# A two-block transformer layer in split fp32: VectorE makes the low weight parts that GpSimd made

## The chip, the cores and the metric

One core of one Trainium2 chip, one launch. The metric is the device time of one execution in microseconds (us); of several runs the median is given. In the profile PE is TensorE's matmul, PEld its weight load, DVE is VectorE, ACT is ScalarE, POOL is GpSimd, and SP is SyncE, which issues most of the DMAs. A small q (SPq, POOLq) marks the queue of an engine.

## The reference, cut to what matters

256 tokens of width 1024, all in fp32, pass through two blocks.

The first block: layer norm; one projection into queries, keys and values of two attentions and into two gates; an 8-head neighbourhood attention and an 8-head windowed attention with a sink; each through its branch matrix; the gated sum

```
mixed = sigmoid(ga) * y_na + sigmoid(gb) * y_swa
h = layer_norm(ALPHA * h + mixed @ w_out + b_out)
h = layer_norm(ALPHA * h + square(relu(h @ w_ff1 + b_ff1)) @ w_ff2 + b_ff2)
```

The second block has two layers. The first mixes by pooling (a trailing mean over 2, 4, 8 or 16 tokens minus the token, then a 256 x 256 matrix for each channel group), the second by a 16-head windowed attention with shared keys and values. After each mixer stands a feed-forward network: a matrix to 2 x 2816 channels, a causal convolution of width 3, gelu(gate) * value, and a matrix back. Norms are RMS norms.

## The kernel before, in words

**Products in three parts.** TensorE runs on a rounded type (fp32r). To keep fp32 accuracy, each weight chunk and each activation is split: the high part is the value rounded to fp32r, the low part is the value minus its high part. A product is the sum of three matmuls, high x high, high x low, low x high (mm3, L364 to L369; in Tm.run, L414 to L432, the order is high x high over all of the contraction, then low weights, then low activations).

**Weights.** The host lays all weights out as 268 chunks of 128 x 1024 in the order of their use. The class Weights (L76 to L175) is the pipeline: load (L91) issues a chunk's DMA on SyncE's queue into a raw buffer; high (L118) makes the high part on ScalarE (L131), and returns a function low, which makes the low part (L141) on the engine that it is given, VectorE by default, then counts the chunk as done and calls load for the next one. There are four raw buffers, and two lent ones at the beginning, so that a load waits for the low part that frees its buffer. For seven chunks a gain is folded in by L129 and L138 instead, always on ScalarE and VectorE. high and low parts live in slots: seven at first (NW), later nine and one extra. take hands the next split chunk to the matmuls, free gives the slot back, and pump(most, eng, keep) splits as many next chunks as there are free slots, most at most, with the low parts on engine eng. highs(n) makes only high parts and leaves the calls of the low parts to the caller.

**Order.** The schedule is written out by hand (manual_schedule): each engine runs its instructions in the order in which the program emits them. An engine that waits for a semaphore holds all its later instructions. So where a low part is called decides what stands behind it on its engine.

**Stages, in order of time.**
- Start: the layer norm ln0 (L495 to L501) of each 128-token half; between the statistics and the centring (L279) it calls mid, which makes the low part of chunk 0. to_fm (L357) transposes on TensorE (L348), copies the high part on ScalarE and subtracts on VectorE (both in split_out, L337 to L339). Tm.run makes the first projections.
- First attention: unit_a (L371 to L388) computes 256 output channels for all tokens; f_va (L569) the values. Scores, softmax and value products are interleaved with the other projections as fillers (step, L727), the branch projection f_bna (L627) among them.
- Branch mixing: the second branch matrix with swa_epi (L766 to L779): L770 reads a PSUM bank, L772 adds two SBUF tensors, ScalarE writes the high part (L775), L777 the low part. Here unit_a is called with ahead=1: high parts are made before the epilogue, low parts after it, for the second half (m = 1) on GpSimd.
- Output projection: Acc.both and Acc.tail (L466 to L489), in which post_ln and to_fm of the first half stand between matmuls; tail's fills names the engines of four low parts. The vector loads of GpSimd's queue (vec, L217) follow the second norm.
- Feed-forward of the first block: GpSimd computes rotary angles meanwhile (rope_angles, L817).
- Pool mixer (L984 to L1071): residual addition L331, scaling L322, transposes, with five low parts between them.
- conv_ffn (L1074 to L1122) for layer 0 and 1: the units 3 to 5 call unit_a with one low part after each half; epilogue L1085 (ScalarE), L1086, L1088, L1093 and the split (VectorE). Four banks rotate, so the matmuls of a unit wait until L1088 of the unit two before has read its bank.
- Second attention (L1204 to L1353): at its end wo is applied to the second half of the tokens, with pump after each chunk (L1351).

The 36 low parts on GpSimd are: chunks 0, 2 and 4 at the start; 10; 13, 15, 17 and 18 in f_va; 31 to 34 in f_bna; 44, 46, 47 and 48 in the branch mixing; 53 in the output projection; 116, 117, 119, 121 and 122 in the pool mixer; 129 to 134 and 214 to 219 in the two conv_ffn; 204 and 206 at the end of the second attention.

Of the kernel before, what the change touches and what calls it, by code (L numbers as in the profile page):

```python
# [177 lines left out]
def model(tc, x_in, wts, bvec, cols_in, const_in, nab_in, pos_in, out):  # L178
    nc = tc.nc
    from contextlib import ExitStack  # L180
    with ExitStack() as top:
# [189 lines left out]
        def unit_a(kx, epi, nk=8, pump=(2, None), ahead=0):  # L371

            cs = [W.take(4, 256) for _ in range(nk // 4)]
            for m in range(2):
                o = bank()
                for k in range(nk):
                    c = cs[k // 4]
                    mm3(o[:, :T], [c[i][:, k % 4, m * P:(m + 1) * P] for i in range(2)], kx(k),
                        k == 0, k == nk - 1, True)
                    if m == 1 and k % 4 == 3:  # L380
                        W.free(cs[k // 4])
                lows = W.highs(ahead)
                later = epi(m, o) or ()
                for low in lows:
                    low((nc.vector,nc.gpsimd)[m])
                W.pump(0 if ahead else pump[0], pump[1], keep=KEEP)
                for f in later:
                    f()  # L388
# [113 lines left out]

        ln0(0, lambda: lows.pop(0)(nc.gpsimd))
        to_fm(x_t[0], xT, 0)
        lows.pop(0)()
        W.pump(1, nc.gpsimd)
        W.pump(1)
        W.pump(1, nc.gpsimd)
        ln0(1, lambda: None, lambda: W.pump(1))
# [50 lines left out]
        W.pump(1)  # L560
        W.pump(1, nc.gpsimd)
        vab = apool.tile([P, 512], F32, name="vab")
# [6 lines left out]
        def f_va():  # L569
            o = [bank() for _ in range(2)]  # L570
            for c in range(4):
                w = W.take(2, 512)
                for t in range(2):
                    for k in range(2):
                        kk = 2 * c + k
                        mm3(o[t], [w[i][:, k, :] for i in range(2)], [a[:, t * P:(t + 1) * P] for a in kx(kk)],
                            kk == 0, kk == 7, False)
                W.free(w)
                (W.pump(1, nc.gpsimd), W.pump(1))
                if c == 1:  # L580
                    yield
            for t in range(2):
                nc.vector.tensor_tensor(out=va[:, t, :], in0=o[t], in1=vab, op=ALU.add)
            yield
# [42 lines left out]
        def f_bna(u):  # L627
            def epi(m, o):
                g = gate["ga", 2 * u + m]
                nc.vector.scalar_tensor_tensor(out=g, in0=g, scalar=1.0, in1=o[:, :T], op0=ALU.add, op1=ALU.mult)  # L630
            unit_a(lambda k: att[k], epi, 4, pump=(1, nc.gpsimd))
            yield
# [170 lines left out]
        for k in range(8 - TAIL):  # L803
# [3 lines left out]
                 lambda: to_fm(h1[0], xT1, 0), 0, 1,(12,2), halves=False,  # L807
                 fills=(nc.vector,nc.gpsimd,nc.vector,nc.vector))
        ctx_g.close()
# [174 lines left out]
        def mid_a():  # L984
            W.pump(2, nc.gpsimd)
            W.pump(1)
# [60 lines left out]
        fb = pool_fm(1, cb)  # L1047
        lows[0](nc.gpsimd)
        for q in range(2):
# [4 lines left out]
        pool_mm(1)  # L1054
        W.pump(1, nc.gpsimd)
        xT2 = new_xt(late)
# [8 lines left out]
        r1 = rms_rstd(ss1)  # L1065
        W.pump(1, nc.gpsimd)
        for q in range(2):
# [6 lines left out]
        def conv_ffn(layer, xt, second, gpost_row, chain_t, after, split):  # L1074
# [30 lines left out]
            for u in range(3, 22):  # L1105
                if u < 6:
                    tm.finish(u - 3, epi_of(u - 3), "b")
                unit_a(kx, epi_of(u), pump=(1, nc.gpsimd) if u < 6 else (2, None))
                if u == 6:
# [235 lines left out]
        for k in range(8):  # L1345
# [4 lines left out]
            if k < 5:  # L1350
                W.pump(1, nc.gpsimd if k % 2 else None)  # L1351
        ctx_a.close()
# [169 lines left out]
```

## Time and profile before

| | |
|---|---|
| three runs, median (lowest, highest) | 896.19 us (894.68, 897.5) |
| the profiled execution | 895.49 us |
| its span in the trace | 893.7 us |
| mean granted TensorE clock | 0.984 of 2.4 GHz |

The profile is of one execution. Its own time holds 1.8 us more than the span, which runs from the first instruction to the last. A row of the timeline gives the start and the duration in us, the engine, the line, the operation, the tiles out<-in, the shape, the count, and in square brackets how long the engine had been idle before it and what ended that. Several equal instructions in a row are merged into one, with their stretch as its duration.

### The profile page before, as it was taken

The numbers are of one execution on the slowest core, as the hardware profiler recorded it, in microseconds if no ns is written. First come the engines' busy times: TensorE is split into PE (matmuls) and PEld (weight loads), VectorE is DVE, ScalarE is ACT, GpSimd is POOL, SyncE is SP. The second block draws the span as 40 slices with busy tenths as digits, with TensorE's granted clock in tenths as the row PEclk, the third lists the DMA queues.
The fourth block names the chain that finished last, engine by engine and source line by source line (L and its number), as shares of the span: only waits on it lengthen the run. The fifth ranks groups of instructions, "written<-read, shape, count | busy, mean of one in ns | idle before, by whom it ended". The sixth has DMA issues, their size and how long they took to land.

```text
span 893.7 us, 15200 instructions
## 1 busy us (share of the span) xinstructions
PE 847.2 (95%) x5872; PEld 764.6 (86%) x5872; DVE 630.2 (71%) x1019; ACT 492.2 (55%) x905; POOL 238.3 (27%) x196
## 2 busy tenths in 40 slices
PE   6999999889899999998999999999999899999997
PEld 5988899768798999788989999988776899999995
DVE  5466754877747755777689877765796678977772
ACT  4555755433535655444666555465786466655551
POOL 4161040323999000343240000046721224000000
PEclk9999999989899999998999999999999999999999
DMA  8683354337635865523447656544152354765531
GB/s 316 201 276 117 134 189 140 120 104 237 224 102 184 278 246 189 184 100 118 165 124 253 217 185 213 179 129 130 59 198 99 142 189 149 261 227 186 179 133 47
DMA packets 43897, 154.61 MB, mean 173 GB/s; under 512 B 5009, under 2 KB 5905, under 8 KB 43826
## 3 DMA queue, kind: packets, MB, share of 16 engines
q1 hardware_dynamic: 41616, 146.90, 48.5%
q0 software_dynamic: 1632, 5.93, 2.1%
q8 instruction: 46, 0.75, 0.3%
q10 hardware_dynamic: 578, 0.82, 0.3%
q14 instruction: 25, 0.20, 0.1%
HBM read 152.58 MB, written 1.05 MB: 172 GB/s over the span
## 4 chain that ended last, share of the span: by engine, by line
PE 66%; DVE 14%; issue 6%; ACT 6%; DMA 5%; POOL 2%; DVEq 0%; POOLq 0%; SPq 0%; ACTq 0%
PE bank_a L369 35%; PE bank_b L369 23%; DVE wlo L141 4%; DMA wraw<-wts_dram 4%; PE bank_a L424 3%; ACT whi L131 2%; DVE p L1262 1%; DVE p L698 1%; ACT p L1274 1%; PE bank_a L720 1%; POOL wlo L141 1%; PE bank_b L709 1%; DVE X L331 1%; DMA v<-bvec_dram 1%; PE bank_b L657 1%
## 5 line engine op out<-in xcount | busy, mean ns | idle before, releaser
L141 DVE TENSOR_TENSOR wlo<-wraw,whi 128x1024 fp32r<-128x1024 f32 x225 | 287.1, 1304 | 78.9 <-ACT whi L131 73.3
L369 PE MATMUL bank_a<-xh,whi 128*128 128x256 f32 x1056 | 297.3, 282 | 4.1 <-DVE cv L1088 3.9
L369 PE MATMUL bank_a<-xh,wlo 128*128 128x256 f32 x1056 | 294.3, 279 | 0.7 <-DVE wlo L141 0.5
L369 PE MATMUL bank_a<-xl,whi 128*128 128x256 f32 x1056 | 294.1, 278 | 0.0
L131 ACT ACTIVATE whi<-wraw 128x1024 fp32r<-128x1024 f32 x261 | 265.5, 1050 | 41.3 <-DMA wraw<-wts_dram 35.0
L369 PEld LDWEIGHTS bank_a<-xh,whi 128*128 128x128 f32 x1056 | 200.0, 189 | 9.2 <-ACT whi L131 4.6
L369 PEld LDWEIGHTS bank_a<-xl,whi 128*128 128x128 f32 x1056 | 200.1, 189 | 1.8
L369 PEld LDWEIGHTS bank_a<-xh,wlo 128*128 128x128 f32 x1056 | 200.0, 189 | 1.3 <-DVE wlo L141 1.0
L141 POOL TENSOR_TENSOR wlo<-wraw,whi 128x1024 fp32r<-128x1024 f32 x36 | 93.6, 2617 | 173.2 <-ACT whi L131 74.8
L1085 ACT ACTIVATE cv<-bank_a,cols 128x256 f32<-128x256 f32 x76 | 41.9, 559 | 78.5 <-PE bank_a L369 78.5
L266 POOL TENSOR_TENSOR rstd<-ve,neghalf 128x1 f32<-128x1 f32 x22 | 13.5, 612 | 232.1 <-DVE ve L307 189.8
L369 PE MATMUL bank_b<-wlo,ah 128*128 128x512 f32 x176 | 69.3, 394 | 0.0
L369 PE MATMUL bank_b<-whi,al 128*128 128x512 f32 x176 | 69.0, 392 | 0.0
L369 PE MATMUL bank_b<-whi,ah 128*128 128x512 f32 x176 | 68.5, 389 | 0.0
L1086 DVE SCALAR_TENSOR_TENSOR cv<-bank_a,cols,cv 128x255 f32<-128x255 f32 x76 | 36.5, 481 | 44.5 <-ACT cv L1085 44.3
L869 POOL TENSOR_SCALAR wraw<-wraw,cols 128x256 f32<-128x256 f32 x28 | 29.5, 1074 | 122.9 <-DVE cv L1086 117.4
L369 PE MATMUL bank_b<-whi,uh 128*128 128x512 f32 x128 | 51.3, 401 | 4.4 <-ACT uh L338 4.4
L369 PE MATMUL bank_b<-whi,ul 128*128 128x512 f32 x128 | 51.4, 402 | 1.7 <-DVE ul L339 1.7
L369 PE MATMUL bank_b<-wlo,uh 128*128 128x512 f32 x128 | 51.2, 400 | 0.0
L369 PEld LDWEIGHTS bank_b<-wlo,ah 128*128 128x128 f32 x176 | 33.1, 188 | 6.6
L1088 DVE SCALAR_TENSOR_TENSOR cv<-bank_a,cols,cv 128x254 f32<-128x254 f32 x76 | 36.6, 482 | 2.7
L369 PEld LDWEIGHTS bank_b<-whi,al 128*128 128x128 f32 x176 | 33.0, 188 | 6.3
(200 smaller groups left out, 1365.8 us busy)
## 6 DMA issues: line engine op xcount, KB each, us to landing
wraw<-wts_dram SPq DMA_DIRECT2D x268, 512.0 KB, 4.4
v<-bvec_dram POOLq DMA_DIRECT2D x10, 512.0 KB, 5.9
v<-bvec_dram SPq DMA_DIRECT2D x4, 512.0 KB, 6.8
nab<-nab_dram SPq DMA_DIRECT2D x4, 384.0 KB, 6.2
poolA<-const_dram POOLq DMA_DIRECT2D x1, 544.0 KB, 6.4
scr<-x_dram SPq DMA_DIRECT2D x2, 256.0 KB, 3.3
scr<-x_dram SPq DMA_DIRECT2D x1, 512.0 KB, 10.1
out_dram<-X SPq DMA_DIRECT2D x2, 256.0 KB, 2.1
```

Of the source, the lines that this page charges most:

```text
L131: self.nc.scalar.activation(out=hi, in_=r, func=AF.Copy)
L141: (eng or self.nc.vector).tensor_tensor(out=lo, in0=r, in1=hi.bitcast(F32), op=ALU.subtract)
L266: nc.gpsimd.tensor_tensor(out=r, in0=v, in1=neghalf, op=ALU.pow)
L331: nc.vector.scalar_tensor_tensor(out=x[:, s], in0=junk[:, s], scalar=r, in1=x[:, s], op0=ALU.mult, op1=ALU.add)
L369: nc.tensor.matmul(o, lhsT=l, rhs=r, start=start and i == 0, stop=stop and i == 2)
L424: nc.tensor.matmul(o[:, :256], lhsT=self.kx(k)[b][:, t * P:(t + 1) * P], rhs=self.cs[u][k // 4][a][:, k % 4, :], start=i == 0 and k == 0, ...
L657: nc.tensor.matmul(s[e][:, j * T:(j + 1) * T], lhsT=q[r, j * P:(j + 1) * P], rhs=k[r, :], start=True, stop=True)
L698: nc.vector.tensor_scalar(out=d, in0=d, scalar1=rc[:, e, j:j + 1], scalar2=None, op0=ALU.mult)
L869: nc.gpsimd.tensor_scalar(out=d, in0=d, scalar1=g, scalar2=None, op0=ALU.mult)
L1085: nc.scalar.activation(out=v, in_=o[:, :T], func=AF.Identity, scale=col(c + 2), bias=col(c + 3))
L1086: nc.vector.scalar_tensor_tensor(out=v[:, 1:T], in0=o[:, 0:T - 1], scalar=col(c + 1), in1=v[:, 1:T], op0=ALU.mult, op1=ALU.add)
L1088: nc.vector.scalar_tensor_tensor(out=v[:, 2:T], in0=o[:, 0:T - 2], scalar=col(c), in1=v[:, 2:T], op0=ALU.mult, op1=ALU.add)
```

## The change

Every call that gave GpSimd (nc.gpsimd) as the engine of a low part now gives VectorE or leaves it to the default, which is VectorE. The order in which the program emits the instructions stays. Cut to the changed lines, which are all of it:

```diff
 unit_a, after the epilogue:
-                    low((nc.vector,nc.gpsimd)[m])
+                    low()
 the first layer norm and what follows it:
-        ln0(0, lambda: lows.pop(0)(nc.gpsimd))
+        ln0(0, lambda: lows.pop(0)())
         to_fm(x_t[0], xT, 0)
         lows.pop(0)()
-        W.pump(1, nc.gpsimd)
         W.pump(1)
-        W.pump(1, nc.gpsimd)
+        W.pump(1)
+        W.pump(1)
 before the first attention:
-        W.pump(1, nc.gpsimd)
+        W.pump(1)
 f_va:
-                (W.pump(1, nc.gpsimd), W.pump(1))
+                (W.pump(1), W.pump(1))
 f_bna:
-            unit_a(lambda k: att[k], epi, 4, pump=(1, nc.gpsimd))
+            unit_a(lambda k: att[k], epi, 4, pump=(1, None))
 output projection:
-                 fills=(nc.vector,nc.gpsimd,nc.vector,nc.vector))
+                 fills=(nc.vector,) * 4)
 pool mixer:
-            W.pump(2, nc.gpsimd)
+            W.pump(2)
-        lows[0](nc.gpsimd)
+        lows[0]()
-        W.pump(1, nc.gpsimd)
+        W.pump(1)
-        W.pump(1, nc.gpsimd)
+        W.pump(1)
 conv_ffn:
-                unit_a(kx, epi_of(u), pump=(1, nc.gpsimd) if u < 6 else (2, None))
+                unit_a(kx, epi_of(u), pump=(1, None) if u < 6 else (2, None))
 end of the second attention:
-                W.pump(1, nc.gpsimd if k % 2 else None)
+                W.pump(1)
```

## Rows read from the trace of the kernel before

**Rows 1.** The page: engines' busy time, share, instructions; then the chain's shares.

```profile
PE 847.2 (95%) x5872; PEld 764.6 (86%) x5872; DVE 630.2 (71%) x1019; ACT 492.2 (55%) x905; POOL 238.3 (27%) x196
PE 66%; DVE 14%; issue 6%; ACT 6%; DMA 5%; POOL 2%; DVEq 0%; POOLq 0%; SPq 0%; ACTq 0%
```

**Rows 2.** The page's costliest groups: count, busy us, mean ns, idle before, its releaser.

```profile
L141 DVE TENSOR_TENSOR wlo<-wraw,whi 128x1024 fp32r<-128x1024 f32 x225 | 287.1, 1304 | 78.9 <-ACT whi L131 73.3
...
L141 POOL TENSOR_TENSOR wlo<-wraw,whi 128x1024 fp32r<-128x1024 f32 x36 | 93.6, 2617 | 173.2 <-ACT whi L131 74.8
```

**Rows 3.** Timeline of the start, VectorE, TensorE and GpSimd.

```profile
6.20 1.40 DVE L279 SCALAR_TENSOR_TENSOR scr<-scr,mv,bank_b 128x512 f32<-128x512 f32 x2
...
9.41 1.97 PE L348 MATMUL bank_a<-ident,scr 128*128 128x128 f32 x8 [3.40 <-DVE scr L284]
...
11.31 2.36 POOL L141 TENSOR_TENSOR wlo<-wraw,whi 128x1024 fp32r<-128x1024 f32 x1 [4.40 <-ACT whi L131]
...
12.99 1.29 DVE L339 TENSOR_TENSOR xl<-bank_a,xh 128x512 fp32r<-128x512 f32 x2 [2.97 <-ACT xh L338]
...
18.65 1.28 DVE L291 BATCH_NORM_STATS2 bst<-scr 128x6 f32<-128x512 f32 x2
...
21.59 1.22 DVE L141 TENSOR_TENSOR wlo<-wraw,whi 128x1024 fp32r<-128x1024 f32 x1
...
22.86 0.74 PE L424 MATMUL bank_a<-wlo,xh 128*128 128x256 f32 x4 [0.21 <-DVE wlo L141]
```

**Rows 4.** Timeline of f_va, the low parts of both engines.

```profile
49.51 11.43 POOL L141 TENSOR_TENSOR wlo<-wraw,whi 128x1024 fp32r<-128x1024 f32 x4 [9.07 <-ACT whi L131]
...
50.41 5.92 DVE L141 TENSOR_TENSOR wlo<-wraw,whi 128x1024 fp32r<-128x1024 f32 x2 [3.12 <-ACT whi L131]
```

**Rows 5.** Timeline of the branch mixing: GpSimd, L772 on VectorE, ScalarE's next part.

```profile
162.31 2.39 POOL L141 TENSOR_TENSOR wlo<-wraw,whi 128x1024 fp32r<-128x1024 f32 x1 [32.54 <-DVE mixl L777]
...
162.66 2.31 DVE L772 TENSOR_TENSOR mix<-gb,ga 128x256 f32<-128x256 f32 x1
...
166.25 0.43 DVE L772 TENSOR_TENSOR mix<-gb,ga 128x256 f32<-128x256 f32 x1
...
168.51 2.31 DVE L772 TENSOR_TENSOR mix<-gb,ga 128x256 f32<-128x256 f32 x1
...
181.84 2.95 ACT L131 ACTIVATE whi<-wraw 128x1024 fp32r<-128x1024 f32 x3 [2.13 <-DVE mixl L777]
```

**Rows 6.** Windows: stretch, its length, busy us by engine, PEclk, DMA share, GB/s.

```profile
182.00:189.00 7.00, 6.04 (x15) 4.28 (x15) 4.79 (x5) 4.30 (x5) 0.00 (x0) 0.51 0.69 232
452.00:455.00 3.00, 3.00 (x16) 3.00 (x15) 2.41 (x3) 1.55 (x4) 3.00 (x2) 0.50 0.32 71
```

**Rows 7.** Timeline behind the branch mixing, VectorE, ScalarE and TensorE.

```profile
194.12 3.56 DVE L284 SCALAR_TENSOR_TENSOR scr<-scr,rstd,v 128x512 f32<-128x512 f32 x2
...
202.56 1.06 ACT L131 ACTIVATE whi<-wraw 128x1024 fp32r<-128x1024 f32 x1 [3.14 <-DMA wraw<-wts_dram]
...
230.88 0.80 PE L369 MATMUL bank_b<-whi,uh 128*128 128x512 f32 x1 [4.43 <-ACT uh L338]
```

**Rows 8.** Timeline of the pool mixer, the residual addition on VectorE.

```profile
400.85 3.50 DVE L331 SCALAR_TENSOR_TENSOR X<-scr,rstd,X 128x512 f32<-128x512 f32 x2
```

**Rows 9.** Timeline of the first conv_ffn, VectorE and TensorE.

```profile
442.59 1.18 DVE L1093 TENSOR_TENSOR cv<-cv 128x256 f32<-128x256 f32 x1
...
444.25 2.06 DVE L339 TENSOR_TENSOR al<-cv,ah 128x256 fp32r<-128x256 f32 x1 [0.48 <-ACT ah L338]
...
450.74 0.36 PE L369 MATMUL bank_a<-xh,whi 128*128 128x256 f32 x1 [1.86 <-DVE cv L1088]
```

**Rows 10.** Timeline of the second attention's end, VectorE, ScalarE and TensorE.

```profile
690.67 6.76 DVE L141 TENSOR_TENSOR wlo<-wraw,whi 128x1024 fp32r<-128x1024 f32 x2
...
697.65 1.06 ACT L131 ACTIVATE whi<-wraw 128x1024 fp32r<-128x1024 f32 x1 [5.37 <-DMA wraw<-wts_dram]
...
699.24 1.00 PE L424 MATMUL bank_a<-whi,xh 128*128 128x256 f32 x6 [2.53 <-ACT xh L338]
```

## The prediction

> **What bounds the kernel now.** I read the page first: TensorE is busy 95% of the span, VectorE 71%, GpSimd 27%, and the chain that ended last is two thirds TensorE, while VectorE holds 14% of it and GpSimd 2% [rows 1]. So TensorE sets the pace in the long stretches, and a change on VectorE and GpSimd can count only in the few where TensorE waits for them. The groups of instructions come next. A low part is a subtraction of two SBUF tensors; 225 are made on VectorE at a mean of 1.30 us, and the 36 that the change moves took GpSimd a mean of 2.62 us [rows 2]. The mean hides the point: alone, a low part takes VectorE 1.22 us [rows 3]; in the value projection of the first attention, where four GpSimd low parts run in a row, two on VectorE take 5.92 us together, 2.96 each [rows 4]. In the loop that mixes both attention branches the timeline shows why: the addition L772 takes 0.43 us without a GpSimd low part beside it and 2.31 us with one, and it ends 0.28 us after that low part ends (162.31 + 2.39 = 164.70; 162.66 + 2.31 = 164.97) [rows 5]. A GpSimd low part holds up a VectorE instruction that takes both of its tensors from SBUF until it is done. So a moved low part adds 1.22 us to VectorE and takes away a hold of up to 2 us, and what it is worth depends on what it stands in front of. I then read the timeline at each of the 36.
>
> **The change part by part.** Against the profiled execution, 895.49 us, of which the span is 893.7; the median of the runs lies 0.70 higher. The loads move too: each low part frees a raw buffer, and SyncE's next weight load waits for it.
>
> *Start (low parts 0, 2, 4).* Low part 0 is called between the statistics and the centring of the first layer norm. On GpSimd it waited until 11.31 for its high part, which waited for its weights; VectorE had centred at 6.20 already [rows 3]. On VectorE the centring queues behind it: 11.31 + 1.22 = 12.5 instead of 6.20. Centring (1.40) and output (the same size) end at 15.3, with the first half of the output done at 14.6, when the transposes can begin (9.41 before). They take 1.97, to 16.5; the last ScalarE copy (taken as long as one half of the split, some 0.65) ends at 17.2, and the split on VectorE (half of 1.29) at 17.9. Low parts 1 to 4 follow, 4 x 1.22 = 4.9, to 22.8; then statistics and centring of the second norm, from 18.65 to 21.59 before, 2.94 us, to 25.7; low part 5 ends at 26.9 instead of 22.81. TensorE waited for exactly this one (22.86) [rows 3], so the whole program behind it moves by **+4.0**. TensorE has no surplus later to win that back. Ends: +1.2 (one low part and nothing else) and +6.3 (the whole delay of the centring).
>
> *Single low part 10 and the four of the first branch projection.* Nothing: VectorE's next work there waits for TensorE's results, which are not late. If that cover were gone, 1.22 each, at most 6.
>
> *Value projection (four).* VectorE does six low parts unhindered, 6 x 1.22 = 7.3 from 49.51, to 56.8, where it was done at 50.41 + 5.92 = 56.3 [rows 4]: **+0.3** with a little overlap; ends 0 and +1.2.
>
> *Branch mixing (four), and the output projection behind it (one).* From one L772 to the next it takes 3.59 us with a GpSimd low part (162.66 to 166.25) and 2.26 with a VectorE one (166.25 to 168.51) [rows 5]. That is 1.33 saved, four times; I take 1.2, since the later ones wait longer for their high parts: -4.8. The last L777 lets ScalarE start the next high part at 181.84, after 2.13 us of waiting [rows 5], so all of it reaches TensorE. Next, the granted clock was 0.51 from 182 to 189, the 1.2 GHz level [rows 6], after TensorE had been stopping for this loop; with the stops shortened I expect 2.4 GHz, and of the 6.04 us that TensorE was busy there I take 4 as work that waited for nothing else; half of it is gained: -2.0. Then the norm's output takes 3.56 us instead of twice 0.7, held by the moved low part of the output projection; the low parts after it, the load behind them and the high part that waited 3.14 us for this load (202.56) come 2.2 us earlier still, and with them the vector loads and the wait that ends at 230.88 [rows 7]: -2.2. Together **-9.0**; ends -4.8 (only VectorE's part) and -11.
>
> *Pool mixer (five).* The residual addition takes 3.50 us for two halves [rows 8], 2.1 more than two of 0.7. That goes; the moved low part now stands in front of it, and I allow 0.5 for waiting for its high part: -2.1 + 1.2 + 0.5 = -0.4. Two low parts ahead of a third in front of a statistic cost VectorE some 0.1. **-0.3**; ends +1.7 and -2.1.
>
> *Convolution layer, first three units after the start, in both layers (six each).* Per unit GpSimd's two low parts stretch L1093 to 1.18 and L339 to 2.06 [rows 9], where L772 of the same size takes 0.43 [rows 5]; a wait of 0.48 for ScalarE stands there as well, and one like it ahead of L1086, which the low parts can fill: 0.75 + 1.63 + 0.9 = 3.3 against 2 x 1.22 = 2.4, so -0.9 ahead of the release that TensorE awaits at 450.74 [rows 9]. Behind this wait, of 1.86 us, the clock stood at 0.50 for at least 3.0 us [rows 6]; with half the wait gone I expect no fall: -1.5. **-2.4** per layer, **-4.8** in all; ends -0.9 and -3 per layer.
>
> *Tail of the second attention (two).* Two VectorE low parts take 6.76 us beside two on GpSimd, 3.38 each; the first would end 2.2 earlier. Behind it stand a load, a high part that waited 5.37 us for that load, behind which the copy xh queues on ScalarE, and TensorE, which waited 2.53 us for xh [rows 10]. **-2.2**; ends -1.2 and -2.5.
>
> Sum: +4.0 + 0.3 - 9.0 - 0.3 - 4.8 - 2.2 = **-12.0**, 883.5 us for the profiled execution and 884.2 beside the median of 896.19; I say 884.
>
> **The rivals.** (a) *Only VectorE's own part is gained:* the clock falls as before and the loads, not the held instructions, set the pace behind the mixing. Then -4.8 there and -0.9 per convolution layer: 4.0 + 0.3 - 4.8 - 0.3 - 1.8 - 2.2 = -4.8, 891.4. For it: high parts do wait for loads [rows 7, 10]. Against: those loads are issued behind the very low parts that come earlier.
>
> (b) *The in-order queue gives it back:* wherever a low part waits for ScalarE, norm work waits behind it. With the ends of start (+6.3) and pool mixer (+1.7) and the rest as in (a): 6.3 + 0.3 - 4.8 + 1.7 - 1.8 - 2.2 = -0.5, 895.7, no change. Only start and mixer show such a place. By the Trainium skill ("Perfetto Trace Analysis", section "Identifying the Most-Contended Engine") the engine with the highest share is the one to relieve; the share of TensorE is not touched here, and by that rule too the time would stay. The trace agrees with the rule for the span as a whole and not for the mixing loop, where TensorE waits for VectorE.
>
> (c) *Slower: VectorE becomes the bound.* If the long L772, L339 and L331 do not come from GpSimd's low parts, each moved low part costs its full 1.22 where VectorE is on the path: four in the mixing, four ahead of the two waits in the convolutions, one in the mixer, two in the tail: 11 x 1.22 = 13.4, with the start 17.4, 913.6. It decides from the point at which the hold taken away is shorter than 1.22 us. Against it: the hold seen is 1.9 us, and it ends with GpSimd's instruction. The Trainium skill ("Perfetto Trace Analysis", section "Optimizing Scalar/DVE Operations") holds that handing VectorE's work to GpSimd may pay where VectorE is saturated, and that it may not since the two share a read port to SBUF; the first half speaks for (c), the second against it, and the trace so far bears out the second.
>
> That the change does not do what it says can hardly be: all 36 calls name the engine. But 160 of GpSimd's 196 instructions stay, and the rotary angles and the weight gains among them can go on holding VectorE; I have counted nothing there.
>
> **How the numbers follow.** Forecast 0.61, (a) 0.22, (b) 0.08, (c) 0.09. The forecast's own ends reach from 877 (mixing -11, convolutions -3 each, mixer -2.1, start +2: 7.2 under the sum) to 889 (mixing -6, convolutions -1.5 each: 4.8 over it); with (a) the range is 877 to 891.5 and leaves out under two in ten. Under 0.3%, 2.7 us, a measurement of this kernel can't be told from no change. Faster: 0.61 + 0.22 = 0.83; same 0.08; slower 0.09.
>
> **What would show it.** In the changed profile: no GpSimd L141; VectorE's L141 at 1.22 to 1.25 us mean; L772 never over 0.5; centring of the first norm after 12.5 and TensorE's wait for low part 5 ending near 26.9; first high part behind the mixing at about 181 (4 later, 4.8 earlier); granted clock 1.00 through the output projection and behind the wait of both convolutions. A mean of L141 that stays at 1.30, or a start over 6 us late, would make the forecast wrong.

## The result and the profile after

The changed kernel takes 880.28 us (median of four runs, 879.57 to 888.32), the kernel before 896.73 beside it: a ratio of 0.9838, interval 0.9803 to 0.9872, 16.5 us less by the medians and some 14.5 by the ratio, where 12.0 were forecast. The profiled execution took 879.9 us, its span 878.1, against 895.49 and 893.7.

The page of the changed kernel: engines' busy time, the group of the low parts.

```profile
PE 836.4 (95%) x5872; PEld 754.9 (86%) x5872; DVE 631.0 (72%) x1055; ACT 492.0 (56%) x905; POOL 146.0 (17%) x160
...
L141 DVE TENSOR_TENSOR wlo<-wraw,whi 128x1024 fp32r<-128x1024 f32 x261 | 320.7, 1257 | 83.0 <-ACT whi L131 82.5
```

VectorE makes 36 more low parts, 36 x 1.22 = 44 us of work, and its busy time goes from 630.2 [rows 1] to 631.0. So 43 us went where 44 came: that much of what stood in its rows as busy time was waiting for GpSimd. The mean of L141 falls from 1304 [rows 2] to 1257 ns.

The timeline of the changed kernel, one engine at a time, at the places of [rows 3, 5, 7 to 10].

```profile
12.05 1.23 DVE L141 TENSOR_TENSOR wlo<-wraw,whi 128x1024 fp32r<-128x1024 f32 x1 [6.78 <-ACT whi L131]
13.20 1.40 DVE L279 SCALAR_TENSOR_TENSOR scr<-scr,mv,bank_b 128x512 f32<-128x512 f32 x2
...
15.31 1.97 PE L348 MATMUL bank_a<-ident,scr 128*128 128x128 f32 x8 [9.31 <-DVE scr L284]
...
27.31 0.74 PE L424 MATMUL bank_a<-wlo,xh 128*128 128x256 f32 x4 [1.57 <-DVE wlo L141]
...
167.11 0.42 DVE L772 TENSOR_TENSOR mix<-gb,ga 128x256 f32<-128x256 f32 x1
167.46 1.22 DVE L141 TENSOR_TENSOR wlo<-wraw,whi 128x1024 fp32r<-128x1024 f32 x1
...
181.63 2.96 ACT L131 ACTIVATE whi<-wraw 128x1024 fp32r<-128x1024 f32 x3 [1.19 <-DVE mixl L777]
...
191.75 1.41 DVE L284 SCALAR_TENSOR_TENSOR scr<-scr,rstd,v 128x512 f32<-128x512 f32 x2
...
206.08 1.04 PE L348 MATMUL bank_a<-ident,scr 128*128 128x128 f32 x8
...
224.36 0.49 PE L369 MATMUL bank_b<-whi,uh 128*128 128x512 f32 x1 [2.31 <-ACT uh L338]
...
396.58 1.41 DVE L331 SCALAR_TENSOR_TENSOR X<-scr,rstd,X 128x512 f32<-128x512 f32 x2
...
439.26 0.43 DVE L1093 TENSOR_TENSOR cv<-cv 128x256 f32<-128x256 f32 x1
440.17 0.43 DVE L339 TENSOR_TENSOR al<-cv,ah 128x256 fp32r<-128x256 f32 x1 [0.48 <-ACT ah L338]
...
441.77 0.36 PE L369 MATMUL bank_a<-xh,whi 128*128 128x256 f32 x1 [0.76 <-DVE cv L1088]
...
680.28 4.63 DVE L141 TENSOR_TENSOR wlo<-wraw,whi 128x1024 fp32r<-128x1024 f32 x4
...
686.60 1.23 PE L424 MATMUL bank_a<-whi,xh 128*128 128x256 f32 x8 [0.28 <-ACT xh L338]
```

Every long VectorE row of before is short: L772 0.42 (2.31), L284 1.41 for both halves (3.56), L331 1.41 (3.50), L339 0.43 (2.06), four low parts in 4.63 (two took 6.76). The price stands at the start: the centring is at 13.20 (6.20), and TensorE gets low part 5 at 27.31 (22.86). The stretches of the clock, by the windows view (the number ahead of the DMA share is the granted clock):

```profile
182.00:189.00 7.00, 6.02 (x26) 4.43 (x25) 5.13 (x6) 4.71 (x5) 0.00 (x0) 1.00 0.69 229
224.00:231.00 7.00, 6.64 (x32) 5.37 (x33) 5.66 (x8) 5.96 (x11) 6.50 (x7) 1.00 0.45 142
452.00:455.00 3.00, 3.00 (x29) 3.00 (x28) 2.86 (x7) 2.28 (x4) 0.00 (x0) 1.00 0.69 197
394.00:398.00 4.00, 3.64 (x20) 3.34 (x18) 3.32 (x6) 3.48 (x7) 0.55 (x1) 0.57 0.07 15
```

At 182 TensorE finishes 26 products at 2.4 GHz where it had 15 at 1.2 [rows 6].

ScalarE makes the high parts in the same order in both kernels. The difference between the starts of the same high part in two traces is therefore a clock for the whole program, and its steps show where the time went (minus is a gain):

| stage | expected | after against before | undone by itself |
|---|---|---|---|
| start | +4.0 | +4.5 | -3.6 (in two ways) |
| value projection, singles | +0.3 | 0.0 | 0.0 |
| mixing and output projection | -9.0 | -11.1 | +6.9 and +3.0 |
| pool mixer | -0.3 | -1.2 | +1.6 |
| first convolution layer | -2.4 | -2.5 | +2.2 |
| tail of the second attention | -2.2 | -2.3 | +3.7 |
| second convolution layer | -2.4 | -3.0 | +2.9 |
| sum | -12.0 | -15.6 | |

The last column is from the experiments below. The largest surprise of the table, the mixing, is in what follows the loop; the first high part behind it comes at 181.63 against 181.84 [rows 5], which with the 4.45 lost at the start makes 4.66 gained in the loop itself.

### The profile page after: what moved, and what is told of

The parts are those of the page before. It is cut to its first block, busy times and chain, and to the rows that moved or that the text cites. A ratio compares the mean times of both kernels' runs of the same rounds, so it can differ in the third digit from the quotient of the medians.

```text
span 878.1 us, 15167 instructions
## 1 busy us (share of the span) xinstructions
PE 836.4 (95%) x5872; PEld 754.9 (86%) x5872; DVE 631.0 (72%) x1055; ACT 492.0 (56%) x905; POOL 146.0 (17%) x160
## 4 chain that ended last, share of the span: by engine, by line
PE 68%; DVE 16%; ACT 7%; issue 4%; DMA 3%; POOL 0%; SPq 0%; DVEq 0%; POOLq 0%; ACTq 0%
PE bank_a L369 36%; PE bank_b L369 24%; DVE wlo L141 7%; PE bank_a L424 4%; ACT whi L131 3%; DMA wraw<-wts_dram 2%; DVE p L1262 1%; DVE p L698 1%; ACT p L1274 1%; PE bank_a L348 1%; PE bank_a L720 1%; PE bank_b L709 1%; ACT scr L302 1%; DMA v<-bvec_dram 1%; PE bank_b L657 1%
## 5 line engine op out<-in xcount | busy, mean ns | idle before, releaser
L141 DVE TENSOR_TENSOR wlo<-wraw,whi 128x1024 fp32r<-128x1024 f32 x261 | 320.7, 1257 | 83.0 <-ACT whi L131 82.5
L369 PE MATMUL bank_a<-xh,whi 128*128 128x256 f32 x1056 | 295.9, 280 | 1.9 <-DVE cv L1088 1.7
L369 PE MATMUL bank_a<-xh,wlo 128*128 128x256 f32 x1056 | 292.7, 277 | 0.7 <-DVE wlo L141 0.5
L369 PE MATMUL bank_a<-xl,whi 128*128 128x256 f32 x1056 | 292.5, 277 | 0.0
L369 PEld LDWEIGHTS bank_a<-xh,whi 128*128 128x128 f32 x1056 | 198.4, 188 | 7.3 <-ACT whi L131 2.7
L369 PEld LDWEIGHTS bank_a<-xl,whi 128*128 128x128 f32 x1056 | 198.7, 188 | 1.7
L369 PEld LDWEIGHTS bank_a<-xh,wlo 128*128 128x128 f32 x1056 | 198.4, 188 | 1.3 <-DVE wlo L141 1.3
L369 PE MATMUL bank_b<-wlo,ah 128*128 128x512 f32 x176 | 69.3, 394 | 0.0
L369 PE MATMUL bank_b<-whi,al 128*128 128x512 f32 x176 | 69.0, 392 | 0.0
L369 PE MATMUL bank_b<-whi,ah 128*128 128x512 f32 x176 | 68.5, 389 | 0.0
L369 PE MATMUL bank_b<-whi,uh 128*128 128x512 f32 x128 | 50.3, 393 | 3.2 <-ACT uh L338 3.2
L369 PE MATMUL bank_b<-whi,ul 128*128 128x512 f32 x128 | 50.7, 396 | 2.5 <-DVE ul L339 2.5
L369 PE MATMUL bank_b<-wlo,uh 128*128 128x512 f32 x128 | 50.3, 393 | 0.0
L369 PEld LDWEIGHTS bank_b<-wlo,ah 128*128 128x128 f32 x176 | 33.1, 188 | 6.6
L1088 DVE SCALAR_TENSOR_TENSOR cv<-bank_a,cols,cv 128x254 f32<-128x254 f32 x76 | 36.6, 482 | 2.7
L369 PEld LDWEIGHTS bank_b<-whi,al 128*128 128x128 f32 x176 | 33.1, 188 | 6.3
L369 PEld LDWEIGHTS bank_b<-whi,ah 128*128 128x128 f32 x176 | 33.0, 188 | 6.0
## 6 DMA issues: line engine op xcount, KB each, us to landing
scr<-x_dram SPq DMA_DIRECT2D x1, 512.0 KB, 11.1
```

What stands on the lines that cost most here:

```text
L141: (eng or self.nc.vector).tensor_tensor(out=lo, in0=r, in1=hi.bitcast(F32), op=ALU.subtract)
L369: nc.tensor.matmul(o, lhsT=l, rhs=r, start=start and i == 0, stop=stop and i == 2)
L1088: nc.vector.scalar_tensor_tensor(out=v[:, 2:T], in0=o[:, 0:T - 2], scalar=col(c), in1=v[:, 2:T], op0=ALU.mult, op1=ALU.add)
```

## The experiments

Each is the changed kernel with an edit of its own. "After" is its 880.28 us; the ratios are to the kernel before. Of the runs with an interval, only the mixing's and the last lie clear of after's (0.9803 to 0.9872). For the others the evidence is in the rows, and in the stage in which the starts of the high parts shift, more than in the whole time.

**Low part 0 later, on VectorE.**

```diff
-        ln0(0, lambda: lows.pop(0)())
+        ln0(0, lambda: None)
+        lows.pop(0)()
         to_fm(x_t[0], xT, 0)
```

> The changed kernel, with low part 0 called behind the first layer norm's output instead of between statistics and centring; all 36 low parts stay on VectorE. Theory (the queue: the centring stands behind low part 0, which waits for its weights): the centring is back at about 5 to 6 us, low part 0 ends at 13.3 in front of the split's subtraction, low parts 1 to 4 end at 19.5, TensorE's wait for low part 5 ends at 23.7 instead of 27.31, and the whole program comes 3.5 us earlier: about 876.8 us. Rival (the three low parts more on VectorE, 3 x 1.22 = 3.7, are what the start costs, wherever they stand): the wait ends at 27.3 as before and the time stays at 880.3.

877.26 us, ratio 0.9805 (0.9773 to 0.9837). Timeline of this run, VectorE and TensorE:

```profile
6.25 1.40 DVE L279 SCALAR_TENSOR_TENSOR scr<-scr,mv,bank_b 128x512 f32<-128x512 f32 x2
...
11.61 1.23 DVE L141 TENSOR_TENSOR wlo<-wraw,whi 128x1024 fp32r<-128x1024 f32 x1 [0.93 <-ACT whi L131]
...
23.29 0.74 PE L424 MATMUL bank_a<-wlo,xh 128*128 128x256 f32 x4 [1.33 <-DVE wlo L141]
```

Its weights landed 0.45 us earlier than in the changed kernel's profile (first high part at 10.52 against 10.97); less that, the wait ends 3.6 us earlier, where the theory had 3.6 (27.31 to 23.7). The queue cost the start, not the number of low parts: all three still stand on VectorE. The whole time gained 3.0, since part of it went again at TensorE's wait before uh, which grew from 2.31 to 4.16 us and ended in a fall of the clock; more on it below.

**Low part 0 back on GpSimd.**

```diff
-        ln0(0, lambda: lows.pop(0)())
+        ln0(0, lambda: lows.pop(0)(nc.gpsimd))
```

> The changed kernel, with low part 0 alone back on GpSimd, at its old place; low parts 2 and 4 stay on VectorE. Theory (the queue): centring near 6 us again, low parts 1 to 4 on VectorE end at 19.1, TensorE's wait for low part 5 ends at 23.3 instead of 27.31, so 4.0 us earlier, about 876.3 us. Rival (the count of low parts on VectorE): one low part less there, so 1.2 us earlier only, wait ending at 26.1, 879.1 us.

876.63 us, 0.9802 (0.9772 to 0.9831). TensorE gets low part 5 at 23.66, having waited 0.46 for it; 23.3 was expected, and the first norm's output (L284) had waited for its vector load until 9.80 (8.61 before). 27.31 less 23.66, with weights 0.08 earlier, is 3.6 again. The two runs can't be told apart: which engine makes low part 0 matters little, where it stands on VectorE matters.

**The mixing's four back on GpSimd.**

```diff
-                    low()
+                    low((nc.vector,nc.gpsimd)[m])
```

> The changed kernel, with the four low parts of the branch mixing (second half of each unit) back on GpSimd; the low part in the output projection stays on VectorE. Theory (hold, then clock): L772 takes 2.3 us four times again, the first high part behind the loop starts 4.6 us later than in the changed kernel, the granted clock is at its lower level for some 7 us behind it (2.0 us more), and what follows comes 6.6 to 9 later: about +7.5, 887.8 us. Rival (only VectorE's own part): +4.6, 884.9, with the clock at 1.00. Rival (VectorE the bound, no hold): four times 1.22 less on VectorE, -4.9, 875.4.

889.09 us, 0.9934 (0.9911 to 0.9958): +8.8 by the medians, +6.9 by the two profiled spans (885.0 and 878.1). Timeline, GpSimd and VectorE, then ScalarE:

```profile
166.66 2.39 POOL L141 TENSOR_TENSOR wlo<-wraw,whi 128x1024 fp32r<-128x1024 f32 x1 [78.93 <-DVE mixl L777]
...
167.02 2.31 DVE L772 TENSOR_TENSOR mix<-gb,ga 128x256 f32<-128x256 f32 x1
...
178.36 2.48 POOL L141 TENSOR_TENSOR wlo<-wraw,whi 128x1024 fp32r<-128x1024 f32 x1 [3.46 <-ACT whi L131]
...
179.06 2.06 DVE L777 SCALAR_TENSOR_TENSOR mixl<-mix,mixh 128x256 fp32r<-128x256 f32 x1 [0.48 <-ACT mixh L775]
...
186.27 2.95 ACT L131 ACTIVATE whi<-wraw 128x1024 fp32r<-128x1024 f32 x3 [2.21 <-DVE mixl L777]
```

The first high part behind the loop starts at 186.27 instead of 181.63, 4.64 later, as expected. The hold is not L772's alone: two of the four are L772, at 2.31, and two are L777, at 2.06 and 2.01, whichever two-tensor instruction comes to stand beside the low part. The clock falls only from 189 to 192 (0.50; 0.97 from 182 to 189), not for 7 us, and the steady difference of 6.9 lies at the lower end of the theory's 6.6 to 9. The rivals fall: +4.6 alone is too little, and nothing became faster.

**The output projection's one back on GpSimd.**

```diff
-                 fills=(nc.vector,) * 4)
+                 fills=(nc.vector,nc.gpsimd,nc.vector,nc.vector))
```

> The changed kernel, with only low part 53, the second of the four in the output projection, back on GpSimd. Theory (hold, then loads): the norm's second output half L284 takes about 2.9 us again instead of 0.74, the low parts and loads behind it come 2.2 us later, the vector loads too, and TensorE's wait before the second feed-forward product grows from 2.6 to about 4.8; with a fall of the clock behind it as in the kernel before, +2.2 to +4.4, I say +3.2: 883.5 us. Rival (the wait is set by something else): no change, 880.3.

882.61 us, 0.9865 (0.9838 to 0.9892): +2.3, by the spans +3.1 (881.2). Timeline, and the clock behind the wait:

```profile
191.47 2.56 POOL L141 TENSOR_TENSOR wlo<-wraw,whi 128x1024 fp32r<-128x1024 f32 x1
...
191.67 3.57 DVE L284 SCALAR_TENSOR_TENSOR scr<-scr,rstd,v 128x512 f32<-128x512 f32 x2
...
207.66 1.29 PE L348 MATMUL bank_a<-ident,scr 128*128 128x128 f32 x8 [1.37 <-DVE scr L284]
...
227.58 0.80 PE L369 MATMUL bank_b<-whi,uh 128*128 128x512 f32 x1 [3.57 <-ACT uh L338]
```

```profile
227.00:230.50 3.50, 2.92 (x7) 2.27 (x8) 2.02 (x6) 2.73 (x7) 3.25 (x4) 0.51 0.52 159
```

One hold of 2.16 us (3.57 less 1.41) returns at two later waits of TensorE. The low parts behind the held output come later, and behind them on VectorE the norm output of the second half: TensorE waits 1.37 us for it, where after has no wait (206.08), and is 1.6 behind. Before uh it waits 1.3 longer. The clock at 1.2 GHz behind that costs 1.0 more, which is gone at the next uh: after waits 0.91 there, this run not at all. Here TensorE's clock fell behind a wait of 3.57 us, and in the run with low part 0 later behind one of 4.16; behind waits of 2.31 (after) and of 2.38 and 2.43 (the runs with low part 0 and with the mixing on GpSimd) it stayed at 1.00. The length of the wait alone does not decide it: in the run with the convolutions' twelve back it fell behind one of 2.46 (0.51 from 226 to 229.5).

**Which GpSimd instructions hold VectorE.** In the four second halves of the mixing, each released by the high part (cut):

```diff
+                if ahead and m:
+                    beside()
...
+            if n == 1:
+                nc.gpsimd.tensor_copy(out=va[:, :1], in_=hi[:, :1])
+                nc.gpsimd.memset(va, 0.0)
+            elif n == 2:
+                nc.gpsimd.tensor_copy(out=va, in_=hi)
+            elif n == 3:
+                nc.gpsimd.tensor_tensor(out=va, in0=va, in1=hi, op=ALU.subtract)
+            elif n == 4:
+                nc.gpsimd.tensor_scalar(out=va, in0=hi, scalar1=0.5, scalar2=None, op0=ALU.mult)
```

> The changed kernel, with one more GpSimd instruction of 128 x 1024 in each of the four second halves of the branch mixing, released by that half's high part and writing to a buffer that nobody reads any more (it adds work and leaves none out). The four are, in order: a write of zeros (memset, behind a copy of one column), a copy (one tensor read), a subtraction of two tensors as in a low part, a multiplication by a constant (one tensor read). VectorE's L770 (0.42), L772 (0.43), low part L141 (1.22) and L777 (0.42) run beside them. Theory (GpSimd holds a VectorE instruction only while it reads two tensors itself): beside the first, second and fourth all stay within 0.1 us of these; beside the subtraction L772 takes 2.3, or, if it comes first, the low part 2.9 us. Rival (any large GpSimd instruction on SBUF holds VectorE): L772 or the low part is over 2 us beside all four. Time: one hold, some +1.2, against +5 by the rival.

One execution, 891.59 us, with one instruction of each kind. GpSimd's instruction and the VectorE instruction beside it (L790 and L141 are the old L772 and L141):

```profile
166.93 0.96 POOL L379 MEMSET va<- 128x1024 f32 x1
...
167.06 0.42 DVE L790 TENSOR_TENSOR mix<-gb,ga 128x256 f32<-128x256 f32 x1
...
171.28 1.04 POOL L381 COPY va<-whi 128x1024 f32<-128x1024 f32 x1 [3.39 <-ACT whi L131]
...
171.58 1.01 DVE L790 TENSOR_TENSOR mix<-gb,ga 128x256 f32<-128x256 f32 x1
...
176.40 2.45 POOL L383 TENSOR_TENSOR va<-va,whi 128x1024 f32<-128x1024 f32 x1 [4.08 <-ACT whi L131]
...
176.47 3.46 DVE L141 TENSOR_TENSOR wlo<-wraw,whi 128x1024 fp32r<-128x1024 f32 x1
...
182.62 2.79 POOL L385 TENSOR_SCALAR va<-whi 128x1024 f32<-128x1024 f32 x1 [3.77 <-ACT whi L131]
...
182.67 2.06 DVE L141 TENSOR_TENSOR wlo<-wraw,whi 128x1024 fp32r<-128x1024 f32 x1
```

Both theories miss. Zeros hold nothing; the copy of one tensor does, until it is done (171.58 + 1.01 is 0.27 behind 171.28 + 1.04, the same 0.28 as in [rows 5]); the subtraction holds fully (3.46 is 1.22 + 2.24); the multiplication, also of one tensor, costs the low part 0.84 and lets it end first. So, as far as one instruction of each kind shows, reading from SBUF is the condition, not reading twice. The Trainium skill ("SBUF — State Buffer", section "Who interferes with whom") says just this of a VectorE instruction with two SBUF inputs: it contends with a GpSimd instruction that reads SBUF, and not with one that only writes it. The zeros, the copy and the subtraction agree with it. The same section of the Trainium skill calls the ports that the two share an exclusive lock; the multiplication doesn't agree, since beside its 2.79 us the low part took 2.06 and ended first. The added holds, 0.59 + 2.24 + 0.84 = 3.67, move the first high part behind the loop from 181.63 to 185.44, by 3.8; the other 8 of the 11.7 us of span come behind it, by a clock of 0.66 from 186 to 193, a wait of the same kind before uh (4.4 from product to product), a fall of the clock that after hasn't (0.52 from 375 to 378.5), and the slow stretch told in the last section.

**Another order at the start, and a later scaling.** Cut; ln0_centre makes the statistics and the centring of one half.

```diff
-        lows = W.highs(2)
+        lows = W.highs(1)
...
-        ln0(0, lambda: lows.pop(0)())
+        mr0 = [ln0_centre(t) for t in range(2)]
+        for q in range(2):
+            ln_out(x_t[0], mr0[0], b0, x_t[0], q)
+        lows.pop(0)()
         to_fm(x_t[0], xT, 0)
...
-        for t in range(2):
-            nc.vector.scalar_tensor_tensor(out=h1[t], in0=h1[t], scalar=ALPHA, in1=bff2, op0=ALU.mult, op1=ALU.add)
...
+            if u == 8:
+                for t in range(2):
+                    nc.vector.scalar_tensor_tensor(out=h1[t], in0=h1[t], scalar=ALPHA, in1=bff2, op0=ALU.mult, op1=ALU.add)
```

> The changed kernel with three changes of order and none of engine: at the start both halves' statistics and centring come first, low part 0 behind the first half's output and high part 1 behind the split's copies; and the scaling with the second bias (L907), which waits for a vector load, is moved from ahead of the low parts behind the first projections of the feed-forward to the sixth unit of its loop, since its result is read only after it. Theory (VectorE's queue order): low part 0 is as cheap as in the run that calls it later (-3.5), TensorE's wait for low part 5 (1.6 there) goes, and its first product starts 0.9 earlier, -6.0 together; behind the feed-forward's first projections the low parts run some 2 us earlier and TensorE's wait of 2.6 at 221.8 shrinks below 1.0 and the one of 1.2 behind it goes: -2.0. Total -8, 872.3 us. Rival (that wait is set by the loads' time alone): -6.0, 874.3.

883.18 us, 0.9849 (0.9823 to 0.9875): no gain where 8 us were expected. By the medians it is 2.9 slower than after, by the two profiled spans 0.3 faster (877.8 and 878.1); the intervals overlap, so which it is stays open. VectorE at the start of this run:

```profile
13.82 1.29 DVE L291 BATCH_NORM_STATS2 bst<-scr 128x6 f32<-128x512 f32 x2 [6.79 <-DMA scr<-x_dram]
...
16.77 1.41 DVE L284 SCALAR_TENSOR_TENSOR scr<-scr,rstd,v 128x512 f32<-128x512 f32 x2
```

The second half of x had not landed until 13.8. No wait in the earlier traces had shown this, since VectorE had always come to it later, but the page of after had it, in its list of DMA issues (size, us from issue to landing):

```profile
scr<-x_dram SPq DMA_DIRECT2D x1, 512.0 KB, 11.1
```

SyncE issues this load at 3.61 us in after, so that it lands at 14.7. The statistics, pulled ahead, waited 6.79 us, and the first half's output behind them with them: the mistake of the start, made again. TensorE's transposes begin at 17.57 instead of 15.31. The later scaling paid: the starts of the high parts, 2.57 behind after's ahead of the feed-forward, are 0.10 behind in its middle, 2.5 gained, and both waits before uh are under 1 us.

**The convolutions' twelve back on GpSimd.**

```diff
-                unit_a(kx, epi_of(u), pump=(1, None) if u < 6 else (2, None))
+                unit_a(kx, epi_of(u), pump=(1, nc.gpsimd) if u < 6 else (2, None))
```

> The changed kernel, with the twelve low parts of the two convolution layers' units 3 to 5 back on GpSimd. Theory (hold, then clock): L1093 takes 1.2 and L339 2.1 us beside them, TensorE's wait for L1088 is 1 us longer in each layer, and the granted clock falls to its lower level behind it: +2.5 in the first and +3.0 in the second layer, 885.8 us. Rival (only VectorE's own part): +0.9 each, 882.1. Rival (no hold, VectorE the bound): faster.

885.76 us, 0.9891 (0.9866 to 0.9917): +5.5, spans +5.9 (884.0). Timeline of the first layer, and the clock in the second:

```profile
442.26 4.94 POOL L141 TENSOR_TENSOR wlo<-wraw,whi 128x1024 fp32r<-128x1024 f32 x2 [4.56 <-ACT whi L131]
...
443.19 0.48 DVE L1088 SCALAR_TENSOR_TENSOR cv<-bank_a,cols,cv 128x254 f32<-128x254 f32 x1
443.78 1.16 DVE L1093 TENSOR_TENSOR cv<-cv 128x256 f32<-128x256 f32 x1
445.42 2.06 DVE L339 TENSOR_TENSOR al<-cv,ah 128x256 fp32r<-128x256 f32 x1 [0.48 <-ACT ah L338]
```

```profile
728.00:731.50 3.50, 3.50 (x19) 3.50 (x19) 2.88 (x4) 2.39 (x5) 3.50 (x2) 0.55 0.15 18
```

L1093 and L339 are held as expected; L1088, which reads a PSUM bank, takes its 0.48 beside the same two low parts. In the first layer TensorE waits twice (1.62, and 1.20 from product to product at 451.9, where after has no such wait), the clock stays at 1.00, and the layer costs 2.2. In the second it waits once, 2.01, behind which the clock stands at 0.55 for 3.5 us, and the layer costs 2.9. The remaining 0.9 of the 5.9 is a longer wait at the end of the second attention, where the edit changed nothing.

**Three other places back on GpSimd.** All the changed lines of low part 10, f_va, f_bna, the pool mixer and the second attention's tail, as they were before; of the eight, two:

```diff
-                (W.pump(1), W.pump(1))
+                (W.pump(1, nc.gpsimd), W.pump(1))
...
-                W.pump(1)
+                W.pump(1, nc.gpsimd if k % 2 else None)
```

> The changed kernel, with low part 10, the four of the value projection, the four of the first branch projection, the five of the pool mixer and the two at the end of the second attention back on GpSimd. Told apart by the stage in which the high parts' starts shift against the changed kernel. Theory: 0 (within 0.3) up to the branch mixing, +1.2 across the pool mixer, +2.3 at the end of the second attention, +3.5 in all, 883.8 us. Rival (the mixer as the prediction had it): +0.3 there, 882.9. Rival (VectorE's added work costs wherever it is put): -1.2 to -5 in the value and branch projections.

885.52 us, 0.9889 (0.9859 to 0.9919): +5.2. Up to the mixing no start of a high part differs by over 0.2 us: these nine low parts are free on either engine. The mixer costs 1.6 (1.2 expected), the tail 3.7 (2.3); another 0.5 went in the second attention ahead of it. In the mixer L331 is back at 3.50 us and TensorE's wait for xl behind it at 2.07 (1.01 in after), but the clock is low there too, 0.50 from 394 to 404, for longer than in after: the 1.6 is hold and clock together, and how they share it is not shown. Timeline and clock of the tail:

```profile
682.26 5.89 POOL L141 TENSOR_TENSOR wlo<-wraw,whi 128x1024 fp32r<-128x1024 f32 x2 [1.16 <-ACT whi L131]
...
682.47 6.76 DVE L141 TENSOR_TENSOR wlo<-wraw,whi 128x1024 fp32r<-128x1024 f32 x2
...
690.98 1.22 PE L424 MATMUL bank_a<-whi,xh 128*128 128x256 f32 x4 [2.48 <-ACT xh L338]
```

```profile
691.00:694.50 3.50, 3.50 (x17) 3.50 (x18) 3.44 (x7) 1.68 (x5) 0.55 (x1) 0.52 1.01 413
```

The rows are those of [rows 10] again, TensorE's wait of 2.48 too (2.53 there), and it costs 2.2: TensorE goes on 4.38 later than in after (690.98 and 686.60) and was 2.19 later at the last product ahead of it. But here the clock fell behind it, for 3.5 us, which is the other 1.5. In the kernel before it stayed up behind the same wait: behind waits of this size it falls in some executions and not in others.

**A version of both orders that paid.** Low part 0 later, as in the first run, and the scaling L907 in the loop; the diff is cut.

```diff
-        ln0(0, lambda: lows.pop(0)())
+        ln0(0, lambda: None)
+        lows.pop(0)()
...
+            if u == 8:
+                for t in range(2):
+                    nc.vector.scalar_tensor_tensor(out=h1[t], in0=h1[t], scalar=ALPHA, in1=bff2, op0=ALU.mult, op1=ALU.add)
```

> The changed kernel with the start as in the run that calls low part 0 behind the first norm's output, and with the scaling by the second bias (L907) moved into the feed-forward's loop as in the run that changed both; the second half's statistics stay where they were. Theory (a vector load and a tensor's second half arrive late, and whatever is queued on VectorE behind the wait for them pays): the start gives -3.0 to -3.6, the feed-forward -2.5: about 874.5 us, with TensorE's waits before uh below 1.2. Rival (the gain in the feed-forward came only from arriving there later): 877.3 us, as with the start alone.

875.88 us, 0.9779 (0.9749 to 0.9808): 1.4 over the theory, by the medians. In its trace the start gains 3.6 (and 0.73 by earlier weights) and the feed-forward 3.1 more, with one wait before uh of 0.66 left: the rival falls. Its profiled execution was the slowest of six, 879.6: its clock fell behind a wait of 2.43 for ul (0.57 from 362 to 366), where after's stayed up behind one of 2.54, and 3.2 us went in a slow stretch that the last section tells of.

**And two more moves.** Cut to the two.

```diff
-        lows = W.highs(2)
+        lows = W.highs(1)
...
         to_fm(x_t[0], xT, 0)
-        lows.pop(0)()
+        W.pump(1)
...
-        lows[0]()
         for q in range(2):
             resid_add(r0, X[0], j0, q)
...
         fm_split(fb, dT, 1, (1,))
+        lows[0]()
```

> The kernel of the run beside it, with two more moves: high part 1 is made behind the split's two copies, and low part 119 in the pool mixer is called behind the residual addition and the split instead of ahead of them. Theory: the split's subtractions start 0.5 us earlier at the start, where VectorE is busy without a gap, and TensorE's wait for xl in the mixer (1.6) shrinks by 1.0: -1.5, about 873 us. Rival (the load behind low part 119 comes 2.5 us later and the weights behind it are late): no gain or up to 1.5 slower than the run beside it.

873.32 us, 0.9768 (0.9738 to 0.9798), the lowest of all, though its interval and that of the run beside it overlap widely. At the start nothing is gained: low part 5 reaches TensorE at 23.01 in both. In the mixer TensorE's wait for xl falls from 1.37 to 0.34, and one of 1.46 for L322 stands behind it; the clock stays at 1.00 from 360 to 420, where after has 0.57 from 394 to 398, and the mixer takes 0.7 less than in after, which may be the clock alone. That it beats the changed kernel (0.9838, from 0.9803) is shown, by some 7 us; that the last two moves do is not.

## Why the prediction was right, step by step

The mechanism and every sign held, and the time, 884 forecast and 880.28 measured, lies in the range. Of the signs named ahead one missed narrowly: the mean of L141 is 1257 ns, where 1.22 to 1.25 us were forecast. The 5.0 us that the sum took from the clock (2.0 and twice 1.5) came, but with some luck, since the runs show it falling in one execution and not in another behind like waits. The terms of the lower end add up to 7.0, not 7.2, which changes nothing. The steps:

- *GpSimd's low part holds VectorE's two-tensor instruction to its end:* shown, by the rows of after, by each part put back, and by the kinds of instructions.
- *Start, +4.0:* measured +4.5, of which 0.8 are weights that landed later in this execution (10.97 against 10.18). The working (centring behind low part 0, low part 5 at 26.9, then 27.31) is confirmed by undoing it alone. The end of +6.3 did not come, nor +1.2.
- *Value projection and the singles, +0.3 and 0:* 0.0, shown.
- *Mixing and output projection, -9.0:* -11.1. The three terms were right. By the starts of the same TensorE products in both traces the loop gave -4.65 (for -4.8), though by two holds of L772 and two of L777, not four of L772; the clock from 182 to 189 gave -2.0, as forecast; and the wait that ends at 230.88 fell from 4.43 to 2.31, -2.1 (for -2.2). Left out was another wait of TensorE that hangs on the same held output, for the norm output of the second half. It stood in the kernel before:

```profile
210.09 1.29 PE L348 MATMUL bank_a<-ident,scr 128*128 128x128 f32 x8 [1.36 <-DVE scr L284]
```

  In after the same transposes begin without a wait (206.08), and putting the one low part back brings it back (1.37): some 1.6. The fall of the clock behind uh (0.55 from 229 to 236.5 before, 1.00 after), which no term held either, is worth little: TensorE is 6.5 us ahead of before at the end of that wait, 8.9 behind the fall, and 6.7 again from 278 on in after: after waits 0.91 at the next product with uh (237.37), and before does not wait there.
- *Pool mixer, -0.3:* -1.2, and 1.6 when put back. L331 fell by 2.09 as expected (3.50 to 1.41); the low part ahead of it and its wait for a high part took 1.3 of the 1.7 allowed. That is 0.4 of the 0.9 between the two. Three things stand in no term. The clock falls here in both kernels, from 394 to 398 after (0.57) and for longer before:

```profile
404.00:411.00 7.00, 5.99 (x29) 5.99 (x30) 6.38 (x7) 2.15 (x4) 3.14 (x2) 0.52 0.23 75
```

  L322 was held as well (3.53, now 1.41). Against these, GpSimd's weight gains (L858), which the change left where they were, now hold the split of ul (L339 1.48 us, 0.41 before), and TensorE waits 2.54 for it instead of 1.74. How the rest is shared among them no run shows.
- *Convolutions, -2.4 each:* -2.5 and -3.0, with the clock at 1.00 as forecast [rows 6]; put back, one layer has the fall and the other a second wait.
- *Tail, -2.2:* -2.3.
- *The rivals:* (a), -4.8 in all, is out: -15.6, with no fall of the clock left but a short one in the mixer. (b) was right that the start gives back, and wrong on its size against the rest. (c) is out: VectorE's busy time did not rise. What the prediction left uncounted is there: GpSimd's rotary angles still stretch low parts to 1.4 and some to 1.8 and, in the wait before uh, L890 to 0.95 (0.41 without them), and its weight gains two low parts to 2.3; no run took that away.

Put back one at a time, the parts make 6.9 + 3.0 + 1.6 + 2.2 + 3.7 + 2.9 - 3.6 = 16.7, against 15.6 between the profiles. They need not agree: the falls of the clock come and go with the execution (1.5 in the tail), the weights landed late in after (0.8), and the mixing and the output projection gave more together (11.1) than apart (9.9). The wait before uh is 4.43 us with both on GpSimd, 3.57 and 2.43 with one, 2.31 with neither, and behind the loop the clock was low for 7 us with both and for 3 with the mixing alone.

## What to carry to other kernels

A busy row is not work: compare an instruction's duration beside its neighbour engine with the same one alone, and where it ends a fixed 0.3 us behind the neighbour's end, as it did here, it is a wait. Moving work onto the busier of two engines pays where it takes such holds away from the instruction that TensorE waits for, and costs where the moved instruction waits for a load with finished work queued behind it. Ask of every instruction that is moved ahead when its operand lands. Where its engine comes late no wait tells; the time of the load's issue and its time to landing do.

## What the runs showed of the hardware that was not expected

- A plain copy on GpSimd, which reads one tensor, holds VectorE (L772 1.01 instead of 0.43), zeros don't, and a multiplication by a constant does in part (1.22 to 2.06).
- TensorE can be slower at a shown clock of 1.00. In the profile of the run with both orders its products between 500 and 590 us took 281 ns on the mean, in the run beside it, on the same chip, 276 (groups of L369, time and mean at the end):

```profile
L369 PE MATMUL bank_a<-xh,wlo 128*128 128x256 f32 x134 | 37.7, 281 | 0.0
```

```profile
L369 PE MATMUL bank_a<-xh,wlo 128*128 128x256 f32 x128 | 35.4, 276 | 0.0
```

Between 476 and 622 us the starts of its high parts lose 3.2 us against after's in this way, with no wait to show for it. The same mean of 281 stands in the run with low part 0 on GpSimd from 780 to 860 (277 and 276 in after), and in the run of the four kinds from 500 to 590. Its cause stays open; differences of two or three us between single executions are no evidence of an edit.
